# Hybrid attention and delta-rule block: root norms as GpSimd powers, x normalised in place after the first values, and an output stage that begins with the delta half of two blocks

## The chip, the cores and the metric

The kernel runs on one core of a Trainium2 chip. TensorE (PE) multiplies, VectorE (DVE), ScalarE (ACT) and GpSimd (POOL) do the element-wise work, and SyncE (SP) issues the DMAs. The metric is the device time of one launch in microseconds. Differences of 0.3% (about 2 us) are what a measurement of this kernel can tell.

## The reference

```python
h = rmsnorm(x, norm1_w)                               # x is 1024 tokens x 1024
proj = h @ w_in                                       # 1024 x 4104
sb_q, sb_k, sb_v, sb_z, g_q, g_k, g_v, g_z, g_b, g_a = split(proj)

# 8 heads of 64: stick-breaking attention, strictly causal
z = q @ k.T / 8
attn = exp(log_sigmoid(z) - sum of softplus(z) over the keys between)
o_sb = rmsnorm(attn @ v, per head) * silu(sb_z)

# 4 heads of 128: gated delta rule, in chunks
qkv = silu(causal_conv4(g_q, g_k, g_v)); q, k l2-normalised
S_t = exp(g_t) S_{t-1} (I - beta_t k_t k_t^T) + beta_t k_t v_t^T ; o_t = S_t^T q_t
o_gdn = rmsnorm(o, per head) * silu(g_z)

out = rmsnorm(x + concat(o_sb, o_gdn) @ w_out, final_norm_w)
```

All inputs and outputs are float32.

## The kernel before, in words

Every large product is made of three: each operand is split into a high and a low part that TensorE takes at its fast fp32r rate (`wqh` and `wql`, `xh` and `xl`), and `mm3` adds high x high, high x low and low x high in PSUM. x lies transposed in SBUF as `xh` and `xl`, eight tiles k of 128 features by 1024 tokens.

**Order.** The program is recorded through a planner (`Model`, `interleave`). Streams, which are Python generators, hand out TensorE work; the planner keeps a clock with estimated durations and fixes, engine by engine, the order in which the instructions stand. Priorities (`DELTA` 0, `WEIGHTS` 2, `BANK` 5, `OUTPUT` 15 to 20, `RESULT` 20) decide between instructions that are ready. On the chip each engine then works through its own list in order, so an engine that falls behind the plan makes the others wait at a fixed place. All recorded instructions carry line 315 in the profile.

**Start.** x is loaded transposed (`xr<-xT`) and split into `xh`, `xl`, scaled by the gain `n1` but not by the root norm of the tokens, with the eight q products in eight PSUM banks meanwhile. Then x is loaded again in natural layout for its squares; `_rsqrt` (a bit trick and three Newton steps on DVE) gives `rstd`. `q_evac` empties the banks. `values(0)` computes the first half of the attention values and the gates `ga`, one block of 128 tokens after the other in two banks, and in between `diagonal` and `row_scale` spread `rstd` along the free axis into `rbc` through four matmuls (`pz<-dg,sm`).

**Projections** then run as the stream of lowest priority that fills TensorE: delta-rule heads `G0` to `G3` (each as key, query and value), keys `k0` to `k3`, gates `z0` to `z7`, the second half of the values `v1`. Each gives two halves of 512 tokens in the two banks `pp`. Because x isn't normalised, every evacuation (`k_evac`, `z_evac`, `g_evac`) begins with a DVE multiplication of the bank by `rbc`: `pre<-pp,rbc`, `zt<-pp,rbc`, `kt<-pp,rbc`. GpSimd makes the low part of the weights (`wel`), of the keys (`kt`) and the product of the gates (`zt<-zt,zs`).

**Delta rule and attention** run beside the projections: `gdn_pre`, `gdn_inv`, `gdn_chain`, and `window`, in which ACT takes two sigmoids of the scores, DVE a running product (`cc`), GpSimd their product (`sg`), and TensorE transposes and multiplies with the values (`po<-ah,v2a`).

**Output.** `out_weights` splits the eight tiles of `w_out` (`woh`, `wol`), `mixed` loads a block's attention half (`o_s`), gates and delta half (`og_s`), normalises both halves on DVE, `prepare` transposes (`pz<-step,mx`), multiplies by the gate (`mf`) and splits (`mh`, `ml`), and `product` multiplies with `w_out` into `pp`. For block 0 the four attention tiles come first; `mixed` waits until the last attention head has left the block's window. The final root norm is `_rsqrt1`: eight DVE steps on one column.

Of the kernel before, what the change touches and what calls it, by code (L numbers as in the profile page):

```python
# [10 lines left out]
F32 = mybir.dt.float32  # L11
# [17 lines left out]
ORDER = "v0 G0 v1 G1 k0 G2 G3 k1 k2 z0 z1 k3 z2 z3 z4 z5 z6 z7".split()  # L29
# [24 lines left out]
def _rsqrt1(V, y, a, h, u):  # L54
    V.tensor_scalar(y.bitcast(I32), a.bitcast(I32), -0.5, float(0x5F3759DF), ALU.mult, ALU.add)
    V.tensor_scalar(h, a, -0.5, None, ALU.mult)
    for _ in range(3):
        V.scalar_tensor_tensor(u, y, h, y, ALU.mult, ALU.mult)
        V.scalar_tensor_tensor(y, u, 1.5, y, ALU.add, ALU.mult)


class Op:


    def __init__(self, eng, ins, cost, prio, seq, table):
        self.eng, self.ins, self.cost, self.prio, self.seq, self.table = eng, ins, cost, prio, seq, table
        self.waits, self.ready, self.end, self.users, self.followers, self.begun = 0, 0.0, None, [], [], False
        self.port = False
# [69 lines left out]
class Model:  # L138
# [108 lines left out]
    def arrive(self, op):  # L247
        heapq.heappush(self.heads[op.eng], (op.prio, op.seq, op))
        if not self.busy[op.eng]:
            self.start(op.eng)  # L250
# [97 lines left out]
def cost(eng, name, args, kw):  # L348
# [17 lines left out]
    if eng == "G":  # L366
        if name == "tensor_tensor":
# [55 lines left out]
def block(tc, xT_d, x_d, n1_d, wE_d, wQ_d, wC_d, conv_d, alog_d, dtb_d, mixw_d, wo_d, fnw_d, out_d):  # L423
# [4 lines left out]
    with ExitStack() as top:  # L428
# [28 lines left out]
        rbc = cst.tile([P, T], F32, name="rbc")  # L457
# [11 lines left out]
        og_s = dr.tile([NB, P, GH, P], F32, name="og_s")  # L469
        cum_s = dr.tile([2, GH, NB, P], F32, name="cum_s")  # L470
# [13 lines left out]
        n1 = s0.tile([P, NK], F32, name="n1")  # L484

# [29 lines left out]

        def q_evac(pt, i, half):
            t = s0.tile([P, 2, 512], F32, tag="xr", bufs=8, name="xq")
            hi, lo = t[:, 0, :], t[:, 1, :]
            A.activation(hi.bitcast(F32R), pt, AF.Copy)
            V.tensor_tensor(lo.bitcast(F32R), pt, hi, ALU.subtract)  # L520
            S.dma_start(qk_s[i, :, :, half * 512:(half + 1) * 512].rearrange("a p t -> p a t").bitcast(F32), t)
# [13 lines left out]
        for _ in range(8):  # L535
            TE.matmul(qp[7][:, 0:P], ident, ident, start=True, stop=True)
        for k in range(NK):
# [3 lines left out]
            xr = s0.tile([P, T], F32, tag="xr", bufs=8, name="xr")  # L541
            n = 1 if k else 2
            for u in range(n):
                hs, es = slice(u * 512, T // n + u * 512), slice(u * 256, 512 // n + u * 256)
                S.dma_start(xr[:, hs], xT_d[k * P:(k + 1) * P, hs])
                S.dma_start(w[:, es], wQ_d[:, k, es])
# [6 lines left out]
            for j in (range(8) if k else (0, 2, 4, 6, 1, 3, 5, 7)):  # L553
                i, hs = j // 2, slice((j % 2) * 512, (j % 2) * 512 + 512)
                es = slice(i * P, (i + 1) * P)
                mm3(qp[j], wh[:, es], wl[:, es], xh[:, k, hs], xl[:, k, hs], k == 0, k == NK - 1)
        S.dma_start(alog, alog_d.partition_broadcast(P))
        S.dma_start(dtb, dtb_d.partition_broadcast(P))

        for b in range(NB):  # L560
            xr = s0.tile([P, T], F32, tag="xr", bufs=8, name="xr")
            S.dma_start(xr, x_d[b * P:(b + 1) * P, :])
            A.activation(xr, xr, AF.Square, accum_out=ssx[:, b:b + 1])
            wc = s0.tile([P, 520], F32, tag="wcr", bufs=6, name="wcr")
            S.dma_start(wc, wC_d[:, b, :])
            A.activation(chl[b][:, 0, :], wc, AF.Copy)
            V.tensor_tensor(chl[b][:, 1, :], wc, chl[b][:, 0, :].bitcast(F32), ALU.subtract)
        S.dma_start(conv, conv_d)
        S.dma_start(mixw, mixw_d)
        V.tensor_scalar(ssx, ssx, 1.0 / D, EPS, ALU.mult, ALU.add)  # L570
        _rsqrt(V, None, rstd, ssx, NB, ux)
        V.tensor_scalar(rs8, rstd, 0.125, None, ALU.mult)
        V.tensor_scalar(ns8, rstd, -0.125, None, ALU.mult)
        for j in range(8):
            q_evac(qp[j], j // 2, j % 2)
# [5 lines left out]
        def v_evac(pt, b, col, h0):  # L581
            src = pt[:, col:col + 256].rearrange("p (h d) -> p h d", d=SBD)
            v2 = at_.tile([P, 4, 2, SBD], F32R, tag=("al", "ah")[b % 2], bufs=2, name="v2e")
            A.activation(v2[:, :, 0, :], src, AF.Copy, scale=rstd[:, b:b + 1])
            V.scalar_tensor_tensor(v2[:, :, 1, :], src, rstd[:, b:b + 1], v2[:, :, 0, :].bitcast(F32), ALU.mult, ALU.subtract)
            S.dma_start(v_s[b, :, h0:h0 + 4, :, :].bitcast(F32), v2.bitcast(F32))


        V.memset(ones, 1.0)
        G.affine_select(triu, ones, pattern=[[1, P]], compare_op=ALU.is_ge, fill=0.0, base=0, channel_multiplier=-1)  # L590

        def diagonal(dgp, g):
            dg = dgp[:, g % 2].rearrange("p (b t) -> p b t", b=2)
            V.tensor_tensor(dg, ident.unsqueeze(1).to_broadcast([P, 2, P]),
                            rstd[:, 2 * g:2 * g + 2].unsqueeze(2).to_broadcast([P, 2, P]), ALU.mult)
            return dg

        def row_scale(half, dgs):
            rp = pz()
            for g, dg in enumerate(dgs):  # L600
# [22 lines left out]
        def values(part):  # L623
            cs = slice(264 * part, 264 + 256 * part)
            n = 264 - 8 * part
            for b in range(NB):
                if part == 0 and 4 < b < 7:
                    row_scale(b - 5, dgs)
                if part == 0 and 4 <= b < 6:
                    dgp = at_.tile([P, 2, 256], F32, tag="sg0", name="dg")  # L630
                    dgs = [diagonal(dgp, 2 * (b - 4) + g) for g in range(2)]
# [799 lines left out]
```

## Time and profile before

| | |
|---|---|
| median of three runs | 686.16 us (685.35 to 687.07) |
| the profiled execution's own time | 687.01 us |
| its span | 685.3 us |
| busy: PE, DVE, ACT, POOL | 660.8, 521.9, 359.6, 300.9 us |
| mean granted TensorE clock | 0.985 |

The span is the time from the first to the last instruction of the profiled execution. A busy time is the union of an engine's instructions. Matmuls are pipelined: one of 512 columns is recorded with some 390 ns, while the next may start 230 ns after it, so what TensorE loses is seen in the gaps between starts and in the clock that it was granted, rather than in the share of busy time.

### The profile page before, as it was taken

The numbers are of one execution on the slowest core, as the hardware profiler recorded it, in microseconds if no ns is written. First come the engines' busy times: TensorE is split into PE (matmuls) and PEld (weight loads), VectorE is DVE, ScalarE is ACT, GpSimd is POOL, SyncE is SP. The second block draws the span as 40 slices with busy tenths as digits, with TensorE's granted clock in tenths as the row PEclk, the third lists the DMA queues.
The fourth block names the chain that finished last, engine by engine and source line by source line (L and its number), as shares of the span: only waits on it lengthen the run. The fifth ranks groups of instructions, "written<-read, shape, count | busy, mean of one in ns | idle before, by whom it ended". The sixth has DMA issues, their size and how long they took to land.

```text
span 685.3 us, 11896 instructions
## 1 busy us (share of the span) xinstructions
PE 660.8 (96%) x3998; PEld 563.5 (82%) x3998; DVE 521.9 (76%) x1179; ACT 359.6 (52%) x867; POOL 300.9 (44%) x343
## 2 busy tenths in 40 slices
PE   8999999999999997999999999999999995999995
PEld 7889878988878896888888898889888884878885
DVE  5363665646888999898788779988988889898743
ACT  5571258433437765654437667578677854212111
POOL 0002158238534943346646476644356662432211
PEclk9999999999999999899999999999999997999999
DMA  8957258544671364313782534452255465545321
GB/s 306 341 181 271 107 170 282 186 143 137 220 227 51 95 190 149 105 32 127 218 272 77 166 124 126 142 177 71 71 173 185 135 223 184 176 146 185 130 76 62
DMA packets 95101, 110.27 MB, mean 161 GB/s; under 512 B 28416, under 2 KB 60224, under 8 KB 95040
## 3 DMA queue, kind: packets, MB, share of 16 engines
q1 hardware_dynamic: 95040, 109.51, 48.4%
q8 instruction: 32, 0.52, 0.3%
q14 instruction: 29, 0.24, 0.1%
HBM read 74.98 MB, written 34.51 MB: 160 GB/s over the span
## 4 chain that ended last, share of the span: by engine, by line
PE 78%; DVE 7%; issue 5%; ACT 5%; DMA 3%; POOL 2%; SPq 1%; POOLq 0%; ACTq 0%; DVEq 0%
PE pp L315 49%; PE pz L315 22%; PE po L315 5%; PE pc L315 3%; ACT L315 1%; ACT nkv L315 1%; DVE sm L315 1%; DVE pp L315 1%; DMA mx<-og_s 1%; DVE tt L315 1%; DVE cc L315 1%; SPq L315 1%; POOL sg L315 1%; DMA xr<-xT 1%; ACT dt L315 1%
## 5 line engine op out<-in xcount | busy, mean ns | idle before, releaser
L315 PE MATMUL pp<-xh,weh 128*128 128x512 f32 x384 | 159.1, 414 | 0.8 <-DVE ac L315 0.8
L315 PE MATMUL pp<-xh,wel 128*128 128x512 f32 x384 | 150.6, 392 | 0.0
L315 PE MATMUL pp<-xl,weh 128*128 128x512 f32 x384 | 150.2, 391 | 0.0
L315 POOL TENSOR_TENSOR wel<-wer,weh 128x512 fp32r<-128x512 f32 x48 | 63.9, 1333 | 119.8 <-ACT weh L315 119.7
L315 POOL TENSOR_TENSOR sg<-sg,cc 128x128 f32<-128x128 f32 (+3 forms) x64 | 79.9, 1250 | 74.9 <-DVE cc L315 60.2
L315 PEld LDWEIGHTS pp<-xh,wel 128*128 128x128 f32 x384 | 72.1, 188 | 16.1
L315 PEld LDWEIGHTS pp<-xh,weh 128*128 128x128 f32 x384 | 72.3, 188 | 13.8 <-DVE ac L315 1.8
L315 PEld LDWEIGHTS pp<-xl,weh 128*128 128x128 f32 x384 | 72.5, 189 | 10.6
L315 ACT ACTIVATE sg<-pz,rs 128x384 f32<-128x384 f32 (+3 forms) x96 | 54.7, 598 | 11.7 <-PE pz L315 10.8
L315 ACT ACTIVATE ah<-pz 128x512 fp32r<-128x512 f32 (+1 forms) x80 | 44.2, 562 | 26.5 <-PE pz L315 23.6
L315 DVE TENSOR_TENSOR_SCAN cc<-pz,step 128x384 f32<-128x384 f32 (+2 forms) x64 | 53.8, 848 | 4.0 <-ACT pz L315 3.6
L315 DVE TENSOR_TENSOR al<-pz,ah 128x512 fp32r<-128x512 f32 (+1 forms) x80 | 49.9, 630 | 7.5 <-ACT ah L315 7.1
L315 PE MATMUL pp<-woh,mh 128*128 128x512 f32 (+1 forms) x136 | 53.3, 392 | 2.0 <-ACT mh L315 2.0
L315 ACT ACTIVATE pz<-pz,ns 128x384 f32<-128x384 f32 (+3 forms) x96 | 53.4, 578 | 0.0
L315 PE MATMUL pp<-woh,ml 128*128 128x512 f32 (+1 forms) x136 | 52.5, 386 | 0.4 <-POOL ml L315 0.4
L315 PE MATMUL pp<-wol,mh 128*128 128x512 f32 (+1 forms) x136 | 52.5, 386 | 0.0
L315 POOL TENSOR_TENSOR ac<-ac,pre 128x512 f32<-128x512 f32 x24 | 31.0, 1291 | 41.6 <-ACT pre L315 41.5
L315 PE MATMUL pp<-chl,xh 128*128 128x264 f32 (+1 forms) x256 | 47.2, 285 | 1.4 <-DVE v2e L315 1.4
L315 POOL TENSOR_TENSOR ml<-mf,mh 128x512 fp32r<-128x512 f32 x16 | 21.6, 1350 | 56.2 <-ACT mh L315 56.2
L315 PE MATMUL pz<-step,sg 128*128 128x128 f32 x288 | 44.1, 275 | 1.8 <-DVE oe L315 1.6
L315 DVE SCALAR_TENSOR_TENSOR pp<-pre,conv,pp 128x512 f32<-128x512 f32 x48 | 36.1, 752 | 11.5 <-ACT pp L315 10.9
L315 PE MATMUL po<-ah,v2a 128*128 128x256 f32 (+1 forms) x160 | 42.3, 289 | 0.0
(225 smaller groups left out, 1596.0 us busy)
## 6 DMA issues: line engine op xcount, KB each, us to landing
wer<-wE SPq DMA_DIRECT2D x48, 256.0 KB, 4.1
xr<-x SPq DMA_DIRECT2D x16, 512.0 KB, 5.9
g_s<-ac SPq DMA_DIRECT2D x24, 256.0 KB, 2.2
qk_s<-xq SPq DMA_DIRECT2D x8, 512.0 KB, 5.5
v_s<-v2e SPq DMA_DIRECT2D x16, 256.0 KB, 2.1
kq<-g_s SPq DMA_DIRECT2D x16, 256.0 KB, 3.6
v2a<-v_s SPq DMA_DIRECT2D x8, 512.0 KB, 4.2
q<-qk_s SPq DMA_DIRECT2D x8, 512.0 KB, 4.5
```

The source lines that it names most:

```text
L315: ins = f(*args, **kw).ins
```

## The change

What it does, in the order of the program:

- **Loads.** A list `LOADS` sets the order of the first transfers: the natural x comes in between the transposed x, the columns for the values (`c0` to `c7`) after it. The eight transposed tiles stay in SBUF (`xr0` to `xr7`). `rstd` goes to DRAM and comes back spread over all partitions as `rbc`; `diagonal`, `row_scale` and their matmuls are gone.
- **First values.** They run over all eight banks, two k at a time. When a k pair is through, its tile, which DVE has by then multiplied in place by gain and `rbc` (`xr0<-xr0,n1,rbc`), is split again into the same `xh`, `xl`. The first projection `G0` reads the new ones. Six of the eight low parts of the value columns (`chl`) move to GpSimd.
- **Evacuations** no longer multiply by `rbc`. For keys, ACT copies the bank and DVE subtracts; for gates, ACT takes the sigmoid from the bank and DVE multiplies; for the delta rule, ACT copies the bank where DVE multiplied before. GpSimd has no part in the keys and gates any more.
- **Root norms of the output stage** are one GpSimd instruction with the operation pow and the exponent -0.5, in place of a DVE chain: eight of 128x8 (`rsb`), eight of 128x1 (`ry`).
- **Output.** `w_out`'s delta tiles (k 4 to 7) are loaded and split first. `mixed` is cut in `mixed_delta` and `mixed_attention`. `prepare` and `product` begin with the delta halves of blocks 0 and 1 in four banks (`pp`, `pp`, `pc`, `pz`), then their attention halves; blocks 2 to 7 follow whole. `mixed` and `prepare` have a higher priority.

```diff
+LOADS = "k0 k1 x0 k2 x1 x2 k3 x3 x4 k4 x5 k5 x6 x7 k6 k7 c0 c1 s c2 c3 c4 c5 c6 c7".split()
-def _rsqrt1(V, y, a, h, u):
-    V.tensor_scalar(y.bitcast(I32), a.bitcast(I32), -0.5, float(0x5F3759DF), ALU.mult, ALU.add)
-    V.tensor_scalar(h, a, -0.5, None, ALU.mult)
-    for _ in range(3):
-        V.scalar_tensor_tensor(u, y, h, y, ALU.mult, ALU.mult)
-        V.scalar_tensor_tensor(y, u, 1.5, y, ALU.add, ALU.mult)
+        half = cst.tile([P, SBH], F32, name="half")
+        V.memset(half, -0.5)
+        def rsqrt(y, a, n):
+            return G.tensor_tensor(y, a, half[:, 0:n], ALU.pow)
...
+        scale = S.dma_start(rbc, rs_s.rearrange("b p -> (b p)").partition_broadcast(P))
+            (V if b < 2 else G).tensor_tensor(chl[b][:, 1, :], wc, chl[b][:, 0, :].bitcast(F32), ALU.subtract)
+        for k in range(NK):
+            V.scalar_tensor_tensor(raw[k], raw[k], n1[:, k:k + 1], rbc, ALU.mult, ALU.mult)
...
+        vp = [pp(), pp(), pz(), pc(), pz(), pz(), pz(), po()]
+        for k0 in range(0, NK, 2):
+            for b in range(NB):
+                bs = slice(b * P, (b + 1) * P)
+                for k in (k0, k0 + 1):
+                    mm3(vp[b][:, 0:264], xh[:, k, bs], xl[:, k, bs], chl[k][:, 0, 0:264], chl[k][:, 1, 0:264], k == 0, k == NK - 1)
+            for k in (k0, k0 + 1):
+                A.activation(xh[:, k, :], raw[k], AF.Copy)
+                V.tensor_tensor(xl[:, k, :], raw[k], xh[:, k, :].bitcast(F32), ALU.subtract)
...
-                TE.matmul(rp[:, 256 * g:256 * g + 256], ones, dg.rearrange("p b t -> p (b t)"), start=True, stop=True)
-            V.tensor_copy(rbc[:, 512 * half:512 * half + 512], rp)
...
-                first(V.tensor_tensor, kt, pt, rbc[:, hs], ALU.mult)
-                A.activation(hi, kt, AF.Copy)
-                G.tensor_tensor(lo, kt, hi.bitcast(F32), ALU.subtract)
+                first(A.activation, hi, pt, AF.Copy)
+                first(V.tensor_tensor, lo, pt, hi.bitcast(F32), ALU.subtract)
...
-                first(V.tensor_tensor, zt, pt, rbc[:, hs], ALU.mult)
-                A.activation(zs, zt, AF.Sigmoid)
-                r = G.tensor_tensor(zt, zt, zs, ALU.mult)
+                first(A.activation, zs, pt, AF.Sigmoid)
+                first(V.tensor_tensor, zt, pt, zs, ALU.mult)
...
-                first(V.tensor_tensor, pre[:, 3:515], pt, rbc[:, half * 512:(half + 1) * 512], ALU.mult)
+                first(A.activation, pre[:, 3:515], pt, AF.Copy)
...
+            k = (p + 4) % NK
...
+        def mixed_delta(b):
...
+            S.dma_start(mx[:, 512:D], og_s[b].rearrange("p h d -> p (h d)"))
+            for g in range(GH):
...
+                r = V.tensor_scalar(mx[:, gs], mx[:, gs], rsg[:, g, b:b + 1], None, ALU.mult)
...
+        def mixed_attention(b):
...
+            G.tensor_tensor(sq, mx[:, 0:512], mx[:, 0:512], ALU.mult)
...
+            V.tensor_reduce(ss, sq.rearrange("p (h d) -> p h d", d=SBD), AX.X, ALU.add)
+            V.tensor_scalar(ss, ss, 1.0 / SBD, EPS, ALU.mult, ALU.add)
+            rsqrt(rs, ss, SBH)
+            flags[f"ma{b}"] = V.tensor_tensor(o, o, rs.unsqueeze(2).to_broadcast([P, SBH, SBD]), ALU.mult)
...
+            for b, gs in ((0, (1,)), (1, (1,)), (0, (0,)), (1, (0,)), *((b, (0, 1)) for b in range(2, NB))):
...
+            steps = [(0, 1, n) for n in range(2)] + [(1, 1, n) for n in range(2)] + [(0, 0, n) for n in range(2)] + [(1, 0, n) for n in range(2)]
...
-                    _rsqrt1(V, ry, sy[:, 0:1], sy[:, 1:2], sy[:, 2:3])
+                    rsqrt(ry, sy[:, 0:1], 1)
```

Two places show how the instructions now stand.

TensorE at the beginning of the output stage, before: `po` is the last attention product, `pz<-step,o2` and `pz<-step,mx` are transposes of attention output and of block 0, `pp<-woh0` the first output product.

```order
L315 MATMUL po_7081<-al_7113,v2a_6737 128x128
L315 MATMUL pz_7190<-step_65,o2_7135 128x128 x2
L315 MATMUL pz_7200<-step_65,mx_6927 128x128 x4
L315 MATMUL pp_7212<-woh0_6566,mh_7198 128x512
L315 MATMUL pp_7212<-wol0_6567,mh_7198 128x512
```

The same place now; `pp_7091<-xh,wel` is the last matmul of the projections, `mx_6755` and `mx_6762` are blocks 0 and 1, and `mh_6900` is block 0's high part, whose delta half was transposed 46 rows earlier.

```order
L311 MATMUL pp_7091<-xh_106,wel_6867 128x512
L311 MATMUL pz_7183<-step_65,mx_6762 128x128 x4
L311 MATMUL pp_7195<-woh4_6463,mh_6900 128x512
...
L311 MATMUL pp_7195<-woh7_6751,ml_6901 128x512
L311 MATMUL pz_7208<-step_65,mx_6755 128x128 x4
...
L311 MATMUL pc_7249<-woh6_6676,ml_7181 128x512
L311 MATMUL pz_7259<-step_65,mx_6762 128x128 x4
...
L311 MATMUL pz_7288<-woh7_6751,ml_7181 128x512
L311 MATMUL pp_7195<-woh0_7144,mh_6900 128x512
```

The attention's last transposes now stand before the end of the projections, and 48 products of the delta halves stand between the projections and the first product that needs an attention half.

DVE at the passage from the first values to `G0`, before: `sm<-pp` takes the gates out of a bank, `v2e` the values, and the 128x32 rows begin the decays.

```order
L315 TENSOR_SCALAR sm_118<-pp_740,rstd_68 128x8
L315 SCALAR_TENSOR_TENSOR v2e_766<-pp_740,rstd_68,v2e_766 128x4x64
L315 TENSOR_SCALAR sm_118<-pp_770,rstd_68 128x8
L315 TENSOR_TENSOR sm_118<-sm_118 128x32
L315 SCALAR_TENSOR_TENSOR sm_118<-sm_118 128x32
```

The same place now; `xr6` and `xr7` are the raw tiles that are scaled in place, `xl` the low part that `G0` reads.

```order
L311 TENSOR_SCALAR sm_121<-pz_556,rstd_68 128x8
L311 SCALAR_TENSOR_TENSOR xr6_352<-xr6_352,n1_111,rbc_112 128x1024
L311 SCALAR_TENSOR_TENSOR v2e_777<-pz_552,rstd_68,v2e_777 128x4x64
L311 SCALAR_TENSOR_TENSOR v2e_782<-pc_553,rstd_68,v2e_782 128x4x64
L311 TENSOR_SCALAR sm_121<-po_557,rstd_68 128x8
L311 SCALAR_TENSOR_TENSOR xr7_386<-xr7_386,n1_111,rbc_112 128x1024
L311 TENSOR_TENSOR xl_107<-xr6_352,xh_106 128x1024
L311 TENSOR_TENSOR sm_121<-sm_121 128x32
L311 TENSOR_TENSOR xl_107<-xr7_386,xh_106 128x1024
```

Both the scaling and the new split of the last two tiles stand behind reads of the last banks of the values, so they cannot begin before the values are nearly done.

More of the change, by code (lines that the diff above doesn't have):

```diff
@@ L247, in arrive @@
     def arrive(self, op):
+        if op.late:
+            op.late = False
+            return
         heapq.heappush(self.heads[op.eng], (op.prio, op.seq, op))
@@ L557, in block @@
+        ck.prio = 3
         S.dma_start(alog, alog_d.partition_broadcast(P))
         S.dma_start(dtb, dtb_d.partition_broadcast(P))
[L560 to L567, printed above, removed]
@@ L568, in block @@
         S.dma_start(conv, conv_d)
         S.dma_start(mixw, mixw_d)
[L570 to L575, printed above, removed]
+        ck.prio = 0
         def first(f, *args, **kw):
@@ L619, in block, with values @@
         busy = {"w0": 0, "w1": 0, "w2": 0, "w3": 0, "T": 0, "al": 0, "po": 0}
-        def values(part):
-            cs = slice(264 * part, 264 + 256 * part)
-            n = 264 - 8 * part
+        def values():
             for b in range(NB):
[L627 to L631, printed above, removed]
                 yield lambda: ps.room("pp", 2)
```

316 lines of the change are left out of this document (187 added, 129 removed).

## The prediction

> **What bounds the kernel now.** I read the page first, then busy time by stretch, then TensorE's waits, the chain that ended last, and the timeline of the two worst places.
>
> ```profile
> PE 660.8 (96%) x3998; PEld 563.5 (82%) x3998; DVE 521.9 (76%) x1179; ACT 359.6 (52%) x867; POOL 300.9 (44%) x343
> ```
>
> The first line of the page gives the share of the span. TensorE is the bound, so a change pays if it takes matmuls away or closes TensorE's gaps; work that other engines save is worth nothing by itself. Where the gaps lie shows in the table by stretch (us from the start; PE, PEld, DVE, ACT, POOL busy; granted clock; DMA share and GB/s).
>
> ```profile
> 50.00:74.00 24.00, 24.00 (x191) 23.71 (x190) 9.91 (x25) 5.54 (x12) 3.48 (x3) 1.00 0.65 236
> 240.00:280.00 40.00, 35.77 (x202) 30.65 (x201) 36.49 (x96) 22.93 (x75) 17.56 (x25) 0.91 0.51 152
> 560.00:600.00 40.00, 32.38 (x157) 26.18 (x156) 35.91 (x83) 12.28 (x18) 16.20 (x13) 0.87 0.50 170
> 600.00:660.00 60.00, 59.28 (x277) 48.19 (x276) 49.36 (x160) 11.52 (x20) 17.30 (x13) 1.00 0.43 142
> ...
> 570.00:575.00 5.00, 0.44 (x2) 0.20 (x2) 4.96 (x7) 4.28 (x6) 1.26 (x1) 0.79 0.88 297
> 575.00:580.00 5.00, 2.30 (x6) 1.21 (x6) 4.90 (x9) 0.63 (x1) 1.43 (x1) 0.50 0.94 328
> 580.00:585.00 5.00, 4.79 (x17) 3.87 (x18) 3.85 (x15) 0.00 (x0) 1.15 (x2) 0.68 0.00 1
> ```
>
> The first values (50 to 74) and the output stage (600 to 660) have next to no idle TensorE. Two holes stand out: 40 - 35.77 = 4.2 us around 270 and 40 - 32.38 = 7.6 us around 575, and in both the granted clock fell (0.91 and 0.87 in the mean; 0.50 at 575 to 580), so matmuls that did run took twice as long. DVE is nearly full in both (36.49 and 35.91 of 40).
>
> What TensorE did around 575, from the timeline (start, duration, engine, what, idle time and its releaser in brackets):
>
> ```profile
> 569.57 0.27 PE L315 MATMUL po<-al,v2a 128*128 128x128 f32 x1
> 570.88 3.52 DVE L315 SCALAR_TENSOR_TENSOR wol<-wor,mixw,woh 128x1024 fp32r<-128x1024 f32 x2
> 571.51 0.44 PE L315 MATMUL pz<-step,o 128*128 128x128 f32 x2 [1.67 <-ACT o L315]
> 574.66 0.68 DVE L315 TENSOR_TENSOR mx<-mx,rsb 128x512 f32<-128x512 f32 x1
> 575.44 1.08 PE L315 MATMUL pz<-step,mx 128*128 128x128 f32 x4 [3.49 <-DVE ssb L315]
> 577.86 0.63 ACT L315 ACTIVATE mh<-mf 128x512 fp32r<-128x512 f32 x1 [3.01 <-DVE mf L315]
> 578.54 0.79 PE L315 MATMUL pp<-woh,mh 128*128 128x512 f32 x1 [2.02 <-ACT mh L315]
> 583.27 0.40 PE L315 MATMUL pp<-woh,mh 128*128 128x512 f32 x1
> ```
>
> The attention half of block 0 was normalised only at 574.66, behind 3.52 us of `wol` on DVE; transposes, `mf` and `mh` followed one after the other, and full pace came back at 583.27. Around 270:
>
> ```profile
> 267.06 2.17 POOL L315 TENSOR_TENSOR wel<-wer,weh 128x512 fp32r<-128x512 f32 x1
> 268.01 1.24 DVE L315 SCALAR_TENSOR_TENSOR rr<-rru,rr 128x8 f32<-128x8 f32 x1
> 269.17 0.68 DVE L315 TENSOR_TENSOR al<-pz,ah 128x512 fp32r<-128x512 f32 x1
> 269.91 0.44 PE L315 MATMUL pz<-step,o 128*128 128x128 f32 x2 [1.48 <-DVE al L315]
> L315 DVE SCALAR_TENSOR_TENSOR rr<-rru,rr x24: 128/166/1262, 120.9 to 359.5; 128x8 f32<-128x8 f32 x24
> ```
>
> A step on eight columns took 1.24 us where its median (last row, by tile) is 0.166. It ended at 269.25, 20 ns after GpSimd's `wel` (267.06 + 2.17 = 269.23). DVE was held up by GpSimd, and TensorE waited for the `al` behind it.
>
> **The change part by part**, against the profiled execution's 687.01 us (span 685.3), which lies 0.85 us above the median of 686.16; an uncertainty of 2 us (0.3%) hides that.
>
> *Matmuls taken away.* The four `dg` products go; all other products keep their number and shape.
>
> ```profile
> 65.03 1.03 PE L315 MATMUL pz<-dg,sm 128*128 128x256 f32 x4
> 65.70 0.60 PE L315 MATMUL pp<-chl,xh 128*128 128x264 f32 x2
> ```
>
> One of the two pairs (recorded as four) holds TensorE for 65.70 - 65.03 = 0.67 us, so **-1.3 us**, certain, since TensorE is full there.
>
> *The passage from first values to G0.* DVE gains eight scalings of 128x1024 and eight new splits.
>
> ```profile
> L315 DVE SCALAR_TENSOR_TENSOR xl<-xr,n,xh 128x1024 fp32r<-128x1024 f32 x7 | 8.8, 1283 | 2.4 <-ACT xh L315 2.4
> L315 DVE SCALAR_TENSOR_TENSOR wol<-wor,mixw,woh 128x1024 fp32r<-128x1024 f32 x8 | 12.1, 1520 | 2.0 <-ACT woh L315 2.0
> L315 DVE SCALAR_TENSOR_TENSOR v2e<-pp,rstd,v2e 128x256 fp32r<-128x256 f32 x16 | 7.6, 478 | 7.5 <-ACT v2e L315 7.3
> ```
>
> Sixteen at 1.28 is 20.5 us, at 1.52 it is 24.3. DVE was busy for 9.91 of the 24 us there, so 14 us were free, and the rest of the scaling goes before 50 or after 74. What counts is the end: the scaling of tile 6 stands behind the read of the seventh bank, which is full some 0.7 us before the values end (24 us over 192 matmuls is 0.125 each, six per bank). From there, tile 6 scaled, two `v2e`, tile 7 scaled, two new splits: 4 x 1.28 + 2 x 0.48 + some 0.6 for small steps = 6.7 us, or 6.0 after the values' end. `G0` needs tile 7 after seven groups of three matmuls at 0.23 = 4.8 us. The stall is 1.2 us; at 1.52 for each long step 2.2. I take **+1.5**. Above, each of the four long steps could wait out a GpSimd subtraction, 1.33 us each by the `wel` row:
>
> ```profile
> L315 POOL TENSOR_TENSOR wel<-wer,weh 128x512 fp32r<-128x512 f32 x48 | 63.9, 1333 | 119.8 <-ACT weh L315 119.7
> ```
>
> That would be +5. Below, 0.5, if `ga` and `v2e` come sooner. The transfers ahead of this cost nothing, by the stretch from 20 to 40:
>
> ```profile
> 20.00:40.00 20.00, 20.00 (x90) 16.58 (x89) 6.57 (x8) 12.23 (x22) 0.00 (x0) 1.00 0.89 316
> ```
>
> At 90 matmuls in 20 us the 192 q products take 43 us, and the last tile is wanted no sooner than after seven eighths of that, 37 us. All of x twice and the q columns are 10.5 MB, at 316 GB/s 33 us; a tile earlier in the list is put back by at most eight natural x tiles of 1.7 us in the same proportion. The SP queue waits for `rstd` before it issues `rbc`, with `c2` to `c7` behind; those are 1.6 MB, 5 us, and wanted from 56 us on. If this cover failed, TensorE would idle for the difference.
>
> *Evacuations.* DVE loses 24 `pre` multiplications; ACT gets a copy each time; GpSimd loses 24 products of keys and gates:
>
> ```profile
> L315 DVE TENSOR_TENSOR pre<-pp,rbc 128x512 f32<-128x512 f32 x24 | 16.5, 688 | 16.1 <-PE pp L315 16.1
> L315 POOL TENSOR_TENSOR zt<-zt,zs 128x512 f32<-128x512 f32 x16 | 21.2, 1322 | 14.0 <-ACT zs L315 13.2 <-PE pp L315 0.8
> L315 POOL TENSOR_TENSOR kt<-kt,sqh 128x512 fp32r<-128x512 f32 x8 | 11.0, 1380 | 14.0 <-ACT sqh L315 12.8 <-DMA kq<-g_s 1.2
> ```
>
> That is 16.5 us of DVE and 32.2 of GpSimd, none of it on TensorE's path except through holes such as the one at 270. That hole costs 4.2 us idle and, at clock 0.91 over 40 us, 3.6 us of full speed, part of which falls into the idle time: 4.2 to 7.8, take 7. Around it DVE has 3 us less to do in 40 and fewer collisions, but `wel` itself stays and the order is new. I take half, **-3.5**, ends 0 and -7.8. ACT, with 22.93 of 40, carries the copies.
>
> *Beginning of the output.* After the last projection stand four transposes and then 48 products that need only `mh` and `ml` of the delta halves, prepared earlier. A group of 48 goes in
>
> ```profile
> 619.69 11.18 PE pp L315 x48
> ```
>
> 11.2 us by the chain. Behind that cover lie the attention halves of blocks 0 and 1 and the four remaining `wol` (4 x 1.52 = 6.1 on DVE, two `mx<-mx,rsb` and three `mf` of 0.7 each = 3.5): 9.6 us, which fits. The hole as it is: from 569.57 + 0.12 to 583.27 are 13.6 us, in which nine products (2.1) and six transposes (0.7) were done, so 10.8 are lost. Left over may be a wait of block 0's attention transposes, which come 12 products (2.8 us) after block 1's, for `mf` and `mx<-mx,rsb`: some 1.3 us. **-9.5**, ends -8 and -10.8.
>
> *Root norms as powers.* The last block's end:
>
> ```profile
> 679.27 0.72 POOL L315 TENSOR_TENSOR y<-y,fnw 128x256 f32<-128x256 f32 x1 [2.04 <-ACT xr L315]
> 679.42 0.15 DVE L315 TENSOR_SCALAR ry<-sy 128x1 int32<-128x1 int32 x1
> 681.18 0.72 ACT L315 ACTIVATE y<-y,ry 128x512 f32<-128x512 f32 x1 [1.99 <-issue]
> L315 POOL TENSOR_TENSOR tm<-xs,br 128x120 f32<-128x120 f32 (+14 forms) x60 | 18.4, 307 | 4.5 <-DMA br<-bd 0.6 <-issue 0.3
> ```
>
> The chain took 681.18 - 679.42 = 1.8 us. The power stands behind `y<-y,fnw`, which ends at 679.99; no power is in this trace. At 0.3 us (the small product, last row) and 0.2 for the way to ACT the end comes 0.7 earlier; it breaks even at 1.0 us and at 2 us costs +1. One column is nearer to the small product: **-0.3**. The 128x8 powers lie in the output stage, where TensorE takes 11.2 us a block and GpSimd `sq` and two `ml` (some 4 us); they cost nothing below 7 us for a block's two powers.
>
> Sum: -1.3 + 1.5 - 3.5 - 9.5 - 0.3 = -13.1, so **674 us**.
>
> **A rule against the change.** The row of 1.24 us is what the Trainium skill, SBUF — State Buffer, section SBUF: two separate sides, states as a rule: a DVE instruction with two SBUF inputs and a GpSimd instruction exclude each other for their whole length. The trace agrees at 268.01. The change replaces operations that read a bank by 16 that read two SBUF operands, in the very stretch where GpSimd now splits six `chl`. By the rule every one of the four long steps at the passage may block, which is the upper end of +5; by the row of free scalings (1.28) it is +1.2.
>
> **The rivals.** (1) *The middle gives nothing.* DVE stays near 36 of 40 and a new order has its own unlucky place. The output still gains: 687 - 1.3 + 1.5 - 9.5 - 0.3 = 677.4; with a second hole like that at 270 it is 684. Chance 0.24. (2) *The output's cover breaks.* The remaining `wol` or the attention halves come late, as `wol` did at 570.88, and 6 of the 9.5 us return: 674 + 6 to 687 - 1.3 + 1.5 = 680 to 687. Against it, the 48 products. Chance 0.08, half of it no change. (3) *The passage locks up*, on the slow side. If all eight GpSimd subtractions there (six `chl`, two `wel`, 1.33 each = 10.7) are waited out by DVE before tile 7 is split, the stall is 1.5 + 10.7 = 12.2, and the clock then falls as from 575 to 585, where 0.50 x 5 + 0.32 x 5 = 4.1 us of full speed went: 16.3 - 1.3 - 0.3 - 9.5 = +5.2, **692**. It decides from a stall of 7 us on, with tile 7's low part 12 us after the values' end. Against it: the six `chl` are needed by 68 us, and come before. Chance 0.08. It is the rule of the Trainium skill above carried to its end. (4) *Powers are slow*: at 10 us for a block's two, GpSimd needs 14 a block against 11.2, seven blocks long: +20 - 13 = +7, 694. Chance 0.04. (5) *The change does not do what it says*, the new order merely shuffling the same waits: 686. Chance 0.03.
>
> **How the numbers follow.** The forecast has 0.53: its own span is from -1.3 + 0.5 - 7.8 - 10.8 - 0.7 = -20.1 (667) to -1.3 + 5 - 8 + 1 = -3.3 (684). Rival 1 lies inside that, and the lower half of rival 2. The range 666 to 684 therefore holds 0.53 + 0.24 + 0.04 = 0.81. Faster by over 0.3% (below 684.1): 0.81. Within 0.3%: half of rival 2 and rival 5, 0.07. Slower: rivals 3 and 4, 0.12.
>
> **What would show it.** Right: no `dg`; TensorE's idle time from the last `pp<-xh,wel` to the first `pp<-woh` under 1 us and the clock at 1.00 there; a stall of 1 to 2 us for `xl` in the first `G0`; the 268 us hole smaller. Wrong: a stall for `xl` over 5 us, a hole before `pp<-woh0`, POOL's `rsb` above 5 us, or a new hole with half clock elsewhere.

## The result: 12 us faster, as forecast, but all of it from the output stage

The changed kernel takes 675.09 us (median of four runs, 673.73 to 675.63) against 685.75 for before on the same chip: ratio 0.9828, 95% interval 0.9813 to 0.9842 (the two medians by themselves give 0.9845, or 10.7 us). On a second chip it was 675.15 against 687.40, ratio 0.9818 (0.9791 to 0.9845). The profiled execution took 674.73 us, its span 673.0. Against before's profiled 687.01 that is -12.3; the sum of the prediction was -13.1.

The first line of the page and the busy time by stretch of the changed kernel (columns as in the prediction):

```profile
PE 657.2 (98%) x3990; PEld 561.6 (83%) x3990; DVE 492.9 (73%) x1016; ACT 380.1 (56%) x899; POOL 298.5 (44%) x341
```

```profile
50.00:74.00 24.00, 24.00 (x186) 23.36 (x185) 23.31 (x21) 13.42 (x20) 12.61 (x6) 1.00 0.73 264
240.00:280.00 40.00, 37.64 (x219) 32.47 (x217) 33.78 (x84) 26.54 (x78) 22.12 (x40) 1.00 0.46 132
280.00:320.00 40.00, 38.12 (x291) 32.16 (x292) 33.27 (x84) 22.94 (x65) 14.21 (x11) 0.91 0.36 96
560.00:600.00 40.00, 40.00 (x209) 33.46 (x208) 31.62 (x58) 14.79 (x24) 22.60 (x17) 1.00 0.52 171
600.00:660.00 60.00, 60.00 (x279) 49.25 (x278) 33.99 (x55) 11.00 (x19) 26.02 (x23) 1.00 0.40 136
```

The hole of the output stage is gone: 40.00 of 40 at clock 1.00, where it was 32.38 at 0.87. The middle still has its hole, now across 280: 2.4 us idle in one stretch, 1.9 in the next, and the clock at 0.91. DVE is full in the first values, 23.31 of 24 us.

To see where the 12.3 us come from, the span is cut at four matmuls: the first value product, the first product of `G0`, the last projection product, the last output product. Before (rows of the timeline):

```profile
50.37 0.40 PE L315 MATMUL pp<-chl,xh 128*128 128x264 f32 x2
75.56 0.39 PE L315 MATMUL pp<-xh,weh 128*128 128x512 f32 x1
568.57 0.40 PE L315 MATMUL pp<-xh,wel 128*128 128x512 f32 x1
677.91 0.28 PE L315 MATMUL pp<-woh,ml 128*128 128x256 f32 x1
```

The changed kernel:

```profile
53.08 0.40 PE L311 MATMUL pp<-chl,xh 128*128 128x264 f32 x2
76.51 0.40 PE L311 MATMUL pp<-xh,weh 128*128 128x512 f32 x1
570.66 0.39 PE L311 MATMUL pp<-xh,wel 128*128 128x512 f32 x1
666.09 0.28 PE L311 MATMUL pp<-woh,ml 128*128 128x256 f32 x1
```

Up to `G0` the change is 0.95 us later, the middle is 1.1 us longer, the output 13.9 shorter (109.34 to 95.42), the tail 0.5 shorter. Before, 1.6 us of attention products and transposes stood after the last projection that now stand ahead of it, so for like work the middle changed by -0.5 and the output by -12.3. The 0.95 contains a slow beginning of that execution: its first matmuls came 0.43 us apart (the timeline's first q products), twice the usual time, until 10.7 us.

```profile
7.29 0.63 PE L311 MATMUL pz<-xh,wqh 128*128 128x512 f32 x1
7.72 0.63 PE L311 MATMUL pz<-xl,wqh 128*128 128x512 f32 x1
```

The same cuts in every kernel that was run, each from its one profiled execution. "Ratio" is against before on the same chip, from all executions.

| kernel | ratio (95% interval) | `G0` begins | middle | output | tail |
|---|---|---|---|---|---|
| before | 1 | 75.56 | 493.0 | 109.3 | 7.4 |
| the change | 0.9828 (0.9813-0.9842) | 76.51 | 494.2 | 95.4 | 6.9 |
| the change, again | 0.9818 (0.9791-0.9845) | 76.03 | 493.8 | 95.4 | 6.9 |
| x's half alone | 1.0004 (0.9988-1.0019) | 75.21 | 494.6 | 106.8 | 7.6 |
| output's half alone | 0.9970 (0.9954-0.9986) | 76.03 | 493.4 | 105.9 | 6.7 |
| same, `wol` first | 0.9945 (0.9917-0.9974) | 78.03 | 494.0 | 104.5 | 6.7 |
| same, z7's product on DVE | 0.9876 (0.9842-0.9911) | 76.06 | 494.3 | 99.0 | 6.7 |
| the change, z7 as before | 0.9957 (0.9941-0.9974) | 76.14 | 495.7 | 105.0 | 6.9 |
| the change, DVE root norms | 0.9892 (0.9865-0.9919) | 76.34 | 495.7 | 99.7 | 7.6 |
| the change, delta powers | 0.9879 (0.9858-0.9900) | 76.45 | 498.0 | 95.3 | 6.9 |
| the change, `tt` on GpSimd | 0.9824 (0.9799-0.9849) | 76.83 | 495.9 | 95.3 | 6.9 |
| the change, columns early | 0.9881 (0.9835-0.9926) | 76.97 | 501.6 | 95.3 | 6.9 |
| the change, quick `rstd` | 1.0112 (1.0077-1.0147) | 75.00 | 516.8 | 95.3 | 6.7 |
| both of these with `tt` | 0.9997 (0.9975-1.0020) | 74.87 | 509.5 | 95.3 | 6.7 |

In the last row "these" are quick `rstd` and `tt` on GpSimd. An output stage in which TensorE never waits takes 95.3 us, so that column shows each kernel's loss there directly (in `before` and in x's half alone it also holds some 1.6 and 0.4 us of work that the others do earlier).

### The profile page after: what moved, and what is told of

Its sections match the earlier page's. It is cut to its first block, busy times and chain, and to the rows that moved or that the text cites. A ratio compares the mean times of both kernels' runs of the same rounds, so it can differ in the third digit from the quotient of the medians.

```text
span 673.0 us, 11808 instructions
## 1 busy us (share of the span) xinstructions
PE 657.2 (98%) x3990; PEld 561.6 (83%) x3990; DVE 492.9 (73%) x1016; ACT 380.1 (56%) x899; POOL 298.5 (44%) x341
## 3 DMA queue, kind: packets, MB, share of 16 engines
q1 hardware_dynamic: 96272, 110.04, 50.4%
## 4 chain that ended last, share of the span: by engine, by line
PE 84%; DVE 7%; ACT 3%; DMA 2%; issue 2%; POOL 0%; POOLq 0%; SPq 0%; ACTq 0%; DVEq 0%
PE pp L311 51%; PE pz L311 24%; PE po L311 6%; PE pc L311 3%; DVE xl L311 1%; DMA wcr<-wC 1%; DMA nb<-bd 1%; DVE xr L311 1%; DVE tt L311 1%; DVE cc L311 1%; DMA n<-n 0%; ACT L311 0%; DVE al L311 0%; DVE rru L311 0%; DVE xq L311 0%
## 5 line engine op out<-in xcount | busy, mean ns | idle before, releaser
L311 POOL TENSOR_TENSOR wel<-wer,weh 128x512 fp32r<-128x512 f32 x48 | 62.5, 1307 | 63.7 <-ACT weh L311 54.8
L311 DVE TENSOR_TENSOR al<-pz,ah 128x512 fp32r<-128x512 f32 (+1 forms) x80 | 50.2, 632 | 12.3 <-ACT ah L311 11.7
L311 ACT ACTIVATE ah<-pz 128x512 fp32r<-128x512 f32 (+1 forms) x80 | 44.1, 560 | 25.4 <-PE pz L311 23.4
L311 ACT ACTIVATE pz<-pz,ns 128x384 f32<-128x384 f32 (+3 forms) x96 | 52.9, 572 | 0.0
L311 PE MATMUL pp<-woh,mh 128*128 128x512 f32 (+1 forms) x120 | 46.0, 383 | 0.0
L311 PE MATMUL pp<-woh,ml 128*128 128x512 f32 (+1 forms) x120 | 45.4, 378 | 0.0
L311 PE MATMUL pp<-wol,mh 128*128 128x512 f32 (+1 forms) x120 | 45.2, 377 | 0.0
L311 PE MATMUL pz<-kh,q 128*128 128x384 f32 (+3 forms) x96 | 36.8, 391 | 4.1 <-DVE al L311 3.6
L311 PE MATMUL po<-al,v2a 128*128 128x256 f32 (+1 forms) x160 | 39.6, 282 | 0.0
```

What stands on the lines that cost most here:

```text
L311: ins = f(*args, **kw).ins
```

## The experiments

**The two halves apart.** `x_alone` has the output stage of before; `out_alone` has the start and the evacuations of before.

```diff
 x_alone:    the changed kernel up to `wts = {}`, before's text behind it
 out_alone:  before's text up to `wts = {}`, the changed kernel's behind it
```

> Only the first half of the change is made: loads, first values in eight banks, x scaled in place, evacuations without the product by rbc. The output stage is word for word that of before, DVE root norms included. Theory A (from the milestones of the two profiles: the start lost 2.7 us, the first values won 1.8, the middle lost 0.2): this half alone is worth nothing, +1 us, between -1 and +3 against before. Theory B (the sum of the prediction): -1.3 + 1.5 - 3.5 = -3.3 us. If A holds, the hole of half clock in the middle is there in some place, and the hole at 570 to 585 us is back with about 12 us lost.

> Only the second half of the change is made: the output stage with its new order and the powers on GpSimd, behind the start, first values and evacuations of before. Theory A (milestones: the output stage got 13.0 us shorter and the tail 0.5): -13.5 us against before, 672.5, as fast as the whole change or faster by 1. Theory B (the prediction): -9.8 us, 676.5. Rival: the new output lives on the DVE time that the other half frees, and without it a hole stays between the last projection and the first output product: -6 us, 680.

x's half alone is worth nothing (687.15 against 687.16), as its Theory A says. The output's half alone is worth 2.1 us, not 9.8 nor 13.5, and not the 6 of the rival either, whose hole is nevertheless there. Together they give 12: the sum of parts fails. Why, the waits of TensorE from 560 us on in `out_alone` tell:

```profile
PE pp L315 <- DVE wol L315: 5.8, 3, 4.0
PE pp L315 <- POOL ml L315: 1.5, 1, 1.5
```

The new order starts with the delta halves in time, but then the attention tiles' `wol` are late: the rival "the output's cover breaks" of the prediction, in a kernel that isn't the one predicted. DVE's timeline, `out_alone` and then the change:

```profile
573.00 1.27 DVE L315 SCALAR_TENSOR_TENSOR wol<-wor,mixw,woh 128x1024 fp32r<-128x1024 f32 x1
585.80 2.47 DVE L315 SCALAR_TENSOR_TENSOR wol<-wor,mixw,woh 128x1024 fp32r<-128x1024 f32 x2
590.28 1.27 DVE L315 SCALAR_TENSOR_TENSOR wol<-wor,mixw,woh 128x1024 fp32r<-128x1024 f32 x1
```

```profile
571.25 0.48 PE L311 MATMUL pp<-woh,mh 128*128 128x512 f32 x1
573.99 1.77 DVE L311 SCALAR_TENSOR_TENSOR wol<-wor,mixw,woh 128x1024 fp32r<-128x1024 f32 x1
580.21 1.27 DVE L311 SCALAR_TENSOR_TENSOR wol<-wor,mixw,woh 128x1024 fp32r<-128x1024 f32 x1
582.66 2.47 DVE L311 SCALAR_TENSOR_TENSOR wol<-wor,mixw,woh 128x1024 fp32r<-128x1024 f32 x2
583.35 0.40 PE L311 MATMUL pp<-woh,mh 128*128 128x512 f32 x1
...
585.68 0.40 PE L311 MATMUL pp<-wol,mh 128*128 128x512 f32 x1
```

In the change the 48 products stand from 571.25 to 583.35, and the fourth `wol` ends only at 582.66 + 2.47 = 585.13. So the 48 alone do not cover it: ten products of block 0's attention half, which need only the earlier `wol`, stand ahead of the first that reads the fourth, at 585.68. With them the cover holds, with 0.55 us to spare.

**`wol` first.** In `out_alone`, the last four splits go ahead of block 2's root norms.

```diff
-            me.other = DELTA + 0.5
+            me.other = DELTA - 0.6
```

> The kernel of the output's half alone (start and evacuations of before) with one priority changed: the last four splits of the output weights go ahead of block 2's root norms on DVE (DELTA - 0.6 instead of DELTA + 0.5). There TensorE stood at 582.8 us for 4.0 us and again at 589 for 1.6 us until wol came, and 8.9 us went with the half clock. Theory A: the output half alone is worth the full 12 to 13 us, and only DVE's order at that place took 9 of them: about 676 us (-11 against before). Theory B: without the other half of the change DVE and GpSimd are too busy there (GpSimd 23.6 of 40 us busy against 14.8 in the whole change, the gates' products among it), and the wait moves to the attention halves mf and ml: 681 to 684 us.

(The 14.8 in that text is ACT's column, read by mistake; GpSimd's in the whole change is 22.6, so the load of GpSimd over 40 us does not tell the two apart.) It came to 683.10 us, Theory B: the four `wol` were done by 581.2 us, and TensorE waited for the half behind them instead, here at 584.28:

```profile
580.07 0.66 PE L315 MATMUL pz<-step,mx 128*128 128x128 f32 x4 [1.33 <-DVE mx L315]
584.28 0.79 PE L315 MATMUL pc<-woh,mh 128*128 128x512 f32 x1 [3.55 <-ACT mh L315]
```

**One product of the last gate.** What of x's half does the output stage need? Two edits, from both sides. The second changes the whole evacuation of z7: a DVE copy (0.69 us) stands where DVE multiplied (0.68), ACT reads the copy, and GpSimd multiplies.

```diff
 out_z7v, on out_alone:
-                r = G.tensor_tensor(zt, zt, zs, ALU.mult)
+                r = (V if i == NK - 1 else G).tensor_tensor(zt, zt, zs, ALU.mult)
 z7_old, on the change, for z7 alone:
-                first(V.tensor_tensor, zt, pt, zs, ALU.mult)
+                first(V.tensor_copy, zt, pt); A.activation(zs, zt, AF.Sigmoid)
+                G.tensor_tensor(zt, zt, zs, ALU.mult)
```

> The kernel of the output's half alone, in which only the last gate z7's product with its sigmoid is moved from GpSimd to DVE. Theory A: what ties the two halves of the change together is GpSimd at the beginning of the output: z7's product (1.28 us, at 578.1 us) stands there ahead of block 1's and 2's sums and powers and holds DVE's four small steps of mx (3.77 us instead of 1.0). Without it the four wol come 2 to 4 us sooner and half of the 8.9 us lost there is back: 679 to 682 us. Theory B: DVE has too much to do in the 11 us of cover in any case, and 0.7 us more on DVE changes nothing or makes it worse: 685 to 687 us.

> The whole change, but the last gate z7 evacuated as before: DVE copies the bank, ACT takes the sigmoid, GpSimd multiplies (the product by rbc is left out, x being normalised). All of the order before z7 stays as it is. Theory A of the run beside it: the cover breaks, wol or the attention halves come late and a hole of 2 to 6 us with half clock stands between 580 and 595 us: 678 to 683 us. Theory B: the cover holds, 675 to 676 us.

Both went as Theory A says, and further. Moved to DVE, that one product takes `out_alone` from a ratio of 0.9970 to 0.9876, some 6.5 us. z7 evacuated as before, with the product on GpSimd, takes the change from 0.9818 to 0.9957, some 9.5 us. In both pairs the change of time sits in the output column. It isn't all that x's half gives: `out_z7v` still loses 3.6 us in the output stage (99.0 against 95.4), where TensorE waits 2.2 us for `wol` and 0.6 for `ml`; no run takes that apart. In `z7_old`, GpSimd's product and DVE's list:

```profile
576.54 1.30 POOL L311 TENSOR_TENSOR zt<-zt,zs 128x512 f32<-128x512 f32 x1
584.63 2.27 DVE L311 SCALAR_TENSOR_TENSOR wol<-wor,mixw,woh 128x1024 fp32r<-128x1024 f32 x1
590.14 0.69 DVE L311 TENSOR_REDUCE ssb<-sq 128x8 f32<-128x512 f32 x1 [1.86 <-POOL sq L311]
590.74 1.67 DVE L311 SCALAR_TENSOR_TENSOR wol<-wor,mixw,woh 128x1024 fp32r<-128x1024 f32 x1
592.46 0.80 PE L311 MATMUL pp<-wol,mh 128*128 128x512 f32 x1 [4.54 <-DVE wol L311]
```

The last two `wol` stand in DVE's list behind a sum that waits for GpSimd's `sq`. So the path is the place of `wol` in the list, which the planner chose anew. The reason given in the expectation, four small `mx` steps held up by GpSimd (3.77 us), is not it: in `out_z7v` the same four took 3.63.

```profile
577.00 3.63 DVE L315 TENSOR_SCALAR mx<-mx,rsg 128x128 f32<-128x128 f32 x4
```

How much is the planner's new order and how much GpSimd's own 1.3 us, these runs don't separate.

**DVE root norms in the output stage.**

```diff
-            rsqrt(rs, ss, SBH)
+            _rsqrt(V, fi, rs, ss, SBH, "rsu")
-                    rsqrt(ry, sy[:, 0:1], 1)
+                    _rsqrt1(V, ry, sy[:, 0:1], sy[:, 1:2], sy[:, 2:3])
```

> The changed kernel with the output stage's powers turned back into the DVE chains of before (ten steps for 128x8, eight for 128x1). Theory A: the powers only shorten the tail, where the chain of eight took 1.8 us against 0.55 for the power plus the way to and from GpSimd; elsewhere TensorE covers both: +0.5 us, 675.5, and no hole. Theory B: the attention halves of blocks 0 and 1 then come late behind the DVE chains, and a hole of 1 to 4 us stands before the third group of output products: 677 to 679 us. The first 12 us of its profile also show whether the half pace of TensorE up to 10.7 us belongs to the new start (then it is here too) or to one execution.

The ratio is 0.9892 against 0.9818 to 0.9828: 4.5 to 5 us slower. This is Theory B's hole of 1 to 4 us, one group of products later than it says; the time, 680.03, lies 1 us above its 677 to 679. The output column shows 4.3 us of it, in waits for `mh` and `ml` of block 1's attention half (1.5 and 0.6 us, and half clock behind them), the tail 0.7. Here too the cover broke (TensorE's waits from 560 us on):

```profile
PE pc L319 <- ACT mh L319: 1.5, 1, 1.5
```

The prices of a power, by tile, in the changed kernel:

```profile
L311 POOL TENSOR_TENSOR rsb<-ssb,half x8: 1636/1651/2537, 570.4 to 628.7; 128x8 f32<-128x8 f32 x8
L311 POOL TENSOR_TENSOR ry<-sy,half x8: 538/550/954, 594.2 to 668.1; 128x1 f32<-128x1 f32 x8
```

And the tail, from the last sum to the scaling of y, in the change and then with DVE's chain: 1.30 and 1.96 us.

```profile
667.40 0.16 DVE L311 TENSOR_TENSOR sy<-sy 128x1 f32<-128x1 f32 x1 [0.58 <-ACT xr L311]
668.12 0.54 POOL L311 TENSOR_TENSOR ry<-sy,half 128x1 f32<-128x1 f32 x1
668.70 0.72 ACT L311 ACTIVATE y<-y,ry 128x512 f32<-128x512 f32 x1 [1.33 <-POOL ry L311]
```

```profile
672.98 0.16 DVE L319 TENSOR_TENSOR sy<-sy 128x1 f32<-128x1 f32 x1 [0.57 <-ACT xr L319]
674.94 0.72 ACT L319 ACTIVATE y<-y,ry 128x512 f32<-128x512 f32 x1 [1.99 <-issue]
```

**The hole in the middle.** In the change it stands at 277 us (timeline):

```profile
268.29 1.54 POOL L311 TENSOR_TENSOR sg<-sg,cc 128x768 f32<-128x768 f32 x1 [3.30 <-DVE sso L311]
268.29 1.56 DVE L311 TENSOR_SCALAR sso<-sso 128x4 f32<-128x4 f32 x1
269.79 1.29 POOL L311 TENSOR_TENSOR wel<-wer,weh 128x512 fp32r<-128x512 f32 x1
269.89 1.21 DVE L311 TENSOR_SCALAR t<-sso 128x4 int32<-128x4 int32 x1
280.59 0.58 DVE L311 TENSOR_TENSOR al<-pz,ah 128x384 fp32r<-128x384 f32 x1
281.22 0.80 PE L311 MATMUL pz<-kh,q 128*128 128x512 f32 x1 [3.58 <-DVE al L311]
```

Steps on four columns take as long as the GpSimd instruction beside them, and ten microseconds later `al`, behind a DVE list without a break, ends at 281.17, just before TensorE goes on. Two edits: the ten-step chains of `rr` and `t` become GpSimd powers; the products `tt` of the inverse move to GpSimd.

```diff
 delta_pow:
-            _rsqrt(V, gd, rr..., ss..., 8, "rru")
+            rsqrt(rr..., ss..., 8)
-            _rsqrt(V, gd, t0, sso, 4, "t0u")
+            rsqrt(t0, sso, 4)
 tt_pool:
-                    V.tensor_tensor(t, left..., right..., ALU.mult)
+                    G.tensor_tensor(t, left..., right..., ALU.mult)
```

> The changed kernel, with the two remaining DVE root norm chains of the delta rule (ten steps on 8 columns eight times, ten on 4 columns eight times) as one GpSimd power each. Theory A: the hole at 277 us comes from those small DVE steps, three of which GpSimd held for 3.2 us (1.56, 1.21 and 0.93 us for steps of 0.17) with al behind them; without them the hole goes, and 4 to 6 us of idle time and half clock with it: 669 to 671 us, and no time after 200 us in which the clock is under 0.97 in a stretch of 40 us. Theory B: DVE is simply overbooked where the first attention windows meet the second delta head, so a hole of the same size shows a little earlier or later: 674 to 676 us. GpSimd should need 1.65 us for 8 columns and 1.0 for 4.

> The changed kernel with the products tt of the delta rule's inverse (16 of 128x512, 1.05 us each on DVE) moved to GpSimd; sums and all else stay. Theory A (after the powers in the delta rule left the middle's loss as it was): the hole between 262 and 292 us is DVE booked past 100% where the second head's inverse meets the first attention windows; 4 us less DVE work there take the hole away: -3 to -6 us, and no clock under 0.97. Theory B: DVE is held by GpSimd's instructions, and 16 more of those make it worse: 0 to +4 us, with small DVE steps of over 1 us around the hole.

Neither Theory A holds. `delta_pow` is 678.86 us (ratio 0.9879), slower than the change by some 4 us, though 160 DVE instructions are gone; its powers cost what was expected (1.65 and 1.02 us), and the hole stands between 268 and 279 us, its last part here:

```profile
278.70 0.79 PE L311 MATMUL pp<-xh,weh 128*128 128x512 f32 x1 [2.48 <-DVE ac L311]
```

`tt_pool` is 675.90, no change that the intervals can tell (inside its Theory B), with its hole at 287 to 291 us. Each edit also gave the planner other durations and so a new order, which neither theory took in. What makes the hole is left open.

**The passage into the first values.** The write of `rstd` held up SP (SP's timeline; then the DMA view from 25 to 60 us):

```profile
37.90 0.38 SPq L311 DMA_DIRECT2D rs_s<-rstd  x1
48.87 0.33 SPq L311 DMA_DIRECT2D rbc<-rs_s  x1
49.30 2.97 SPq L311 DMA_DIRECT2D wcr<-wC  x6
```

```profile
rs_s<-rstd SPq DMA_DIRECT2D x1, 4.0 KB, 11.0
```

Four kernels bear on it: the change again (`after_again`); the columns `c2` to `c7` ahead of `rbc` (`early_cols`); `rstd` transposed on DVE and written in pieces of 128 bytes (`fast_rs`); and that together with `tt` on GpSimd (`fast_tt`).

```diff
 early_cols:
-LOADS = "... k6 k7 c0 c1 s c2 c3 c4 c5 c6 c7"
+LOADS = "... k6 k7 c0 c1 c2 c3 c4 c5 c6 c7 s"
 fast_rs:
-        S.dma_start(rs_s.rearrange("b p -> p b"), rstd)
+        V.tensor_copy(r32[:, 0:NB], rstd)
+        V.transpose(rt, r32)
+        for q in range(4):
+            S.dma_start(rs_s[:, 32 * q:32 * q + 32], rt[32 * q:32 * q + NB, :])
```

> The changed kernel once more, word for word, so that the single edits beside it stand against it on the same chip. The half pace of its first matmuls (427 ns a matmul until 10.7 us, 1.8 us lost) is not the change's doing if it is gone here: the first values should then start at 51 to 51.5 us instead of 53.1, as they did in the four kernels above. Time 674 to 676.5 us. The middle hole near 277 us belongs to the program's order and should stand in the same place with the same 3.7 us.

> The changed kernel with one entry of the list LOADS moved: c2 to c7 are issued ahead of the load of rbc instead of behind it. In the changed kernel the write of rstd (4 KB in 1024 pieces) took 11.0 us from its issue at 37.9, rbc waited for it, and the six columns behind rbc, so that GpSimd split them from 55.1 to 67.7 us, beside DVE's scalings, which took 2.3 us instead of 1.28. Theory A: split before 53 us they leave DVE alone, DVE is through its 16 long steps 4 to 6 us sooner, and the waits of the first values and of G0 (0.5 us in the changed kernel, 1.5 to 4 in its variants) go: -0.5 to -2 us. Theory B: DVE is full from 53 to 82 us anyway, and its last step sets G0 as before: 0.

> The changed kernel with rstd turned by a 32x32 transpose on DVE first, so that it goes to DRAM in four transfers of eight pieces of 128 bytes instead of one of 1024 pieces of 4 bytes, which took 11.0 us and held SP's queue from 37.9 to 48.9 us. Theory A: rbc then lands near 45 us instead of 52.9, the columns c2 to c7 behind it come 8 us sooner too, DVE scales in the time in which it was idle (45 to 49 us), and the waits at 54 to 58 us for chl and of the first G0 for xl go. From the first value matmul to G0 23.4 us or less, 24.6 to 25.6 before in the variants that came out of the q products at 51 us; in all -1.5 to -2.5 us, unless the planner's new order in the middle gives or takes some (it did by up to 5 us in the variants). Theory B: DVE's 16 long steps are the limit and nothing changes, 0 plus or minus the middle.

> Both: rstd written in 128-byte pieces, and the products tt of the delta rule's inverse on GpSimd. If the two gains seen or hoped for add up (the start -1.5 to -2.5 us; with tt on GpSimd TensorE lost 6 us less between 300 and 560 us but 3 more around 290), 671 to 674 us. Rival: the middle only trades one hole for another, 675 to 677 us.

The change came out as before, with its hole again at 277.6 us. Its first products were slow again (52.6 us to the first value product), and so they were in `out_wol` (52.9), which has the old start; in the other kernels the first value product came at 50.4 to 51.9, in `x_alone` with the new start at 51.4. So the slow beginning comes and goes with the execution and is no part of the change. The Trainium skill, TensorE: Matmul & The Clock Gate, Part 1: The HAM clock gate, says that the number of slow first matmuls varies from run to run; the rows here agree, at 0.43 us each.

`fast_rs` did at the start half of what Theory A said: `rbc` was issued at 40.53 us instead of 48.87, and the first values took 23.4 us without a wait, where the variants that left the q products at 51 us took 23.8 to 25.6, most of them waiting for `chl` or the evacuation of the q banks. `G0` began at 75.0. But DVE did not scale in its idle time: the first scaling began at 52.37 us (52.88 in the change), since in DVE's list it stands behind the evacuation of the q banks. And the first `G0` waited 2.0 us for `xl`, where the kernels with the slow write waited 1.2 at most (DVE's timeline, then TensorE's waits from 40 to 100 us):

```profile
52.37 1.28 DVE L311 SCALAR_TENSOR_TENSOR xr<-xr,n,rbc 128x1024 f32<-128x1024 f32 x1
PE pp L311 <- DVE xl L311: 2.0, 2, 1.5
```

The middle took 516.8 us, 23 more, its worst wait here, and the whole 695.00:

```profile
122.55 0.80 PE L311 MATMUL pp<-chl,xh 128*128 128x256 f32 x2 [4.83 <-DVE ac L311]
```

`fast_tt` was 687.34 with the same start and a middle of 509.5. `early_cols` was 679.43 with a middle of 501.6 (its profiled execution was its slowest), and no gain at the start. In all three DVE's instructions between 75 and 560 us stand in an order that is largely another than in the change, while in the late edits `z7_old` and `newton` it is almost the same there. So an edit worth 1 us at most at 50 us, with the order that it triggers, moves the next 500 us by up to 23. No version tried beats the change.

## Why the prediction was right in the sum and wrong in its terms

**Start and passage (-1.3 and +1.5): right.** `G0` begins at 75.2 to 77.0 us with the new start, unless `rstd` is quick, and at 75.6 to 76.1 with the old one where the first matmuls weren't slow. The lost `dg` products pay for the waits. The predicted stall of `G0` for `xl` was 0.3 us idle in the change (0.47 between two starts), below the +0.5 end, since TensorE came late to the first values in that execution; it was 1.1 in `x_alone` and 2.0 in `fast_rs`. (The upper end of +5 is the four subtractions, 4 x 1.33, alone; the stall of 1.2 to which they would add makes it 6.5.) The place was right, the chain partly: GpSimd's six `chl` (12.61 us in the 50 to 74 row) ran against DVE's long steps, which took 2.3 us beside them and 1.27 without:

```profile
64.15 2.34 DVE L311 SCALAR_TENSOR_TENSOR xr<-xr,n,rbc 128x1024 f32<-128x1024 f32 x1
71.00 1.27 DVE L311 SCALAR_TENSOR_TENSOR xr<-xr,n,rbc 128x1024 f32<-128x1024 f32 x1
```

The lock rule of the Trainium skill (SBUF — State Buffer, SBUF: two separate sides) was thus at work, as in the third rival, though not to the full: one after the other, 1.27 and the 1.33 of a GpSimd subtraction (the `wel` row of the prediction) would be 2.6. But GpSimd was through at 67.7 us, before tiles 6 and 7. "The transfers ahead of this cost nothing" was nearly wrong: the prediction read bytes and missed the 1024 pieces of the `rstd` write.

**Evacuations (-3.5): wrong.** "Around it DVE has 3 us less to do in 40" came true: 33.78 us between 240 and 280, where it was 36.49. The step that failed is "I take half", which lets TensorE's hole shrink with DVE's load. DVE was busy without a break from 270 to 280, and what it had to do still came too late, in a new order and at another place; what makes that hole is open. Idle time from 240 to 320 was 4.2 + 0.8 us before and is 2.4 + 1.9 now, each time with the clock at 0.91 in one stretch of 40 us. `x_alone` shows this half by itself: 0. The first rival held for the middle, in its unlucky place of the new order, though not in its DVE load near 36 us.

**Beginning of the output (-9.5, ends -8 and -10.8): too small, and its condition was missed.** The waits are gone as argued, and the measured -12.3 lies past the lower end. The 1.3 us kept for a late `mf` didn't arise, and another 0.9 us, not in the sum, was lost before between the product at 605.48 us and the transposes at 606.60; some 0.6 is not traced. The missed part is what the cover needs. The working compared 9.6 us of steps with 11.2 of cover and called it a fit. In the change the steps end 13.9 us after the first product of the cover (571.25 to 585.13): the working left out what DVE does besides, z7's product, the sums of block 1, block 2's root norms and a wait of 1.5 us for GpSimd's power. By that measure the cover fails. It holds because ten products more stand ahead of the last `wol`'s first reader, with 0.55 us left, and it held in none of the four kernels that evacuate z7 in another way. The evacuations' 3.5 us were looked for at 270 us; what the runs show of their worth lies at 575.

**Root norms (-0.3): the size was off.** The tail gained 0.66 us against DVE's chain. A power on one column takes 0.55 us, not 0.3, but from the last sum to the scaling it is 1.30 us with the power and 1.96 with DVE's chain. That they "cost nothing" otherwise was right; that they are needed for the cover, 4.3 us in `newton`, was not seen.

**The sum.** -13.1 predicted, -12.3 measured: an error of +3.0 in the middle and one of -2.8 in the output cancelled. That is luck. Of the signs that the prediction named, the `dg` products are gone and TensorE is not idle ahead of the first output products; the stall for `xl` was 0.3 us and not 1 to 2, and a hole with a slower clock, named as a sign of being wrong, stands at 277 us.

## What to carry to other kernels

When work is hidden behind a cover, add up everything that the covering engines' lists hold in that time, also what isn't new, and name the margin: here it was 0.55 us, and one gate evacuated as before, with a GpSimd product of 1.3 us and the order that the planner then chose, cost 9.5 of the 12 us. Run the halves of a change apart before explaining its gain: 0 and 2 made 12. And where a planner fixes the order from estimated durations, an early edit is measured together with the order that it triggers; late edits, behind which little is left to reorder, give the cleaner answers.

## What was not expected of the hardware

- A write of 4 KB in 1024 pieces of 4 bytes took 11.0 us; in four transfers with pieces of 128 bytes the queue went on after 2.3 us (38.25 to 40.53). The load of `rbc`, 512 KB behind it, took 4.0.
- A power on GpSimd costs about 0.4 us and 0.157 us for each column: 0.55, 1.02 and 1.65 us for 1, 4 and 8 columns.
- DVE steps on four columns with one SBUF input (268.29 and 269.89 above) took 1.56 and 1.21 us, as long as the GpSimd instruction that ran beside them, against 0.17 otherwise.
